# Three changes to the weights of a decoder trunk's feed-forward layers on one core: low parts of plain units by ScalarE and an adding DMA, three plain gate/up pairs instead of four, and one order of sections for both layers

## The chip, the core and the metric

The kernel runs on one core of one Trainium2 chip. The time is the device time of one execution in microseconds (us); the time before is the median of three. The engines are TensorE (PE in the profile, its weight loads PEld), VectorE (DVE), ScalarE (ACT), GpSimd (POOL) and SyncE (SP, which issues DMAs here). SBUF is the on-chip memory of 128 partitions, PSUM the one that TensorE writes, in eight banks of 512 float32 per partition here.

## The reference

The input is x, 512 tokens of 1024 channels, float32. Two layers follow, each a mixer and a dense SwiGLU feed-forward layer, each with an RMS norm ahead and a residual addition behind; a last norm ends it. The mixer of layer 0 is dilated causal attention (24 heads of 128 in three groups), that of layer 1 is causal pooling over 2, 4, 8 and 16 positions in four channel groups. Cut to the part that the change touches:

```
def swiglu_ffn(h, w_gate_up, w_down):          # D_MODEL = 1024, D_FF = 2816
    gu = h @ w_gate_up
    gate, up = gu[..., :D_FF], gu[..., D_FF:]
    return (jax.nn.silu(gate) * up) @ w_down
x = x + swiglu_ffn(rmsnorm(x, ffn_norm[i]), w_ffn_gate_up[i], w_ffn_down[i])
```
and, of the pooling mixer, its input projection `u = h @ w_in` (1024 x 1024).

## The kernel before

**Numbers.** Each float32 operand is split into a high part, rounded to the matmul type fp32r, and a low part, the rest. A product then takes three matmuls: high weight with high and with low data, low weight with high data (L312, L313, L315 for plain products; L444 to L446 for the others). The helper `split` (L91, L92) makes both parts: ScalarE copies the high part, VectorE subtracts it from the value for the low part.

**Weights.** Everything that streams in is planned ahead in three queues: `loads`, `steps`, `units`. A `Plain` unit loads up to 1024 columns by SyncE into one of four `raw` buffers and splits them into one of five `w` buffers (high and low half side by side). A `Pair` unit (Strassen-like, seven products for a 2 x 2 block product) loads two `raw` and one `rawhalf`, adds a block to one of them by an adding DMA from GpSimd's queue (L159), and fills three `w` and one `half` buffer, with two more sums on VectorE (L175, L176). `pump` issues what the rings have room for; it is called behind each product, so a unit is split when the one five places before it in the ring has been used up.

**Products.** A plain product (`Product`) takes 8 chunks of 128 rows with three matmuls of 512 columns each. A product of a pair (`seven`, `chained`) takes seven block products of 4 chunks with three matmuls of 256 columns. In `chained` four of the block products go into a PSUM bank that ScalarE copies out before the next one is added to it (L518, L522, L526, L534).

**The feed-forward layer** (`ffn`). There are 22 chunks of 128 hidden channels. `gate_up(j)` makes chunk j: the first NPLAIN = 4 by two plain products (`plain_pair`), the rest by seven products (`strassen_pair`). During the plain pairs `prepare(k)` (k = 0 to 3) makes the sums and differences of the normed input that the later pairs need, in VectorE and ScalarE. PARTS tells in which sections the second matrix (FF2) is applied: (first, end, block). A section with block is a block product of `chained` form over weights `w_dblock`; one without is plain, eight products of end - first chunks, weights `w_down`. Layer 0 has a plain section of 6 chunks and two blocks of 8, so it ends with a block; layer 1 has a plain section of 2, two blocks of 8, and a plain section of 4 at the end. A section's results are added to x by `down`; behind the last one `note` makes the next norm's operands (ScalarE the high part L376, VectorE the low part L377) and the squares (ScalarE L365, sum L367).

**The norms.** `finish` completes two leading products, whose weights are thereby used up, then calls `rstd`: TensorE sums the squares (L394), VectorE scales (L397), GpSimd takes the power -1/2 (L400, two instructions); TensorE goes on with half a product and then spreads the result (L407). The pooling layer's additions of squares are GpSimd's (`square(..., nc.gpsimd)`), and its input projection comes as eight plain units `w_pin`.

**Order.** Which instruction comes first on an engine's queue is decided when the program is built; the source gives each its dependences and a place. DMAs issued by GpSimd stand in its queue among its arithmetic.

Of the kernel before, what the change touches and what calls it, by code (L numbers as in the profile page):

```python
# [8 lines left out]
F32 = mybir.dt.float32  # L9
F32R = mybir.dt.float32r  # L10
AF = mybir.ActivationFunctionType
OP = mybir.AluOpType
# [3 lines left out]
P = 128  # L16
S = 512
# [19 lines left out]
NF = 4  # L37
H2 = S // 2
K2 = KC // 2
NPLAIN = 4  # L40
WARM = 6
NSOLO = 3
PARTS = {0: ((0, 6, False), (6, 14, True), (14, 22, True)), 1: ((0, 2, False), (2, 10, True), (10, 18, True), (18, 22, False))}
ENDS = 5
BACK = {"blocks": 3, "sums": 7}
BUFS = {"w": 5, "half": 2, "raw": 4, "rawhalf": 2}
# [9 lines left out]
def units_of(n):  # L56
    return (n,) if n <= KC else (n // 2, n - n // 2)
# [3 lines left out]
PIN_ORDER = (6, 7, 4, 5, 2, 3, 0, 1)  # L61
# [3 lines left out]
def trunk(ctx: ExitStack, tc: tile.TileContext, xT, xN, norms, w_first, w_qk, w_qkp, w_v0, w_v0p, w_v12, w_out, w_pair, w_down, w_dblock, w_pin, w_pgrp,  # L65
          consts, ident_in, invcnt_in, outT, outR):
    nc = tc.nc
# [22 lines left out]
    def split(hi, lo, v):  # L90
        nc.scalar.activation(hi, v, AF.Copy)  # L91
        nc.vector.tensor_tensor(lo, v, hi.bitcast(F32), op=OP.subtract)  # L92
# [27 lines left out]
    class Plain:  # L120


        def __init__(self, *srcs, shift=0):
            self.srcs, self.n, self.w, self.shift = srcs, sum(src.shape[-1] for src in srcs), None, shift
            loads.append((self, {"raw": 1}, self.load))
            steps.append((self, "w", self.split))

# [6 lines left out]

        def split(self):
            self.w = Held("w", self.shift)
            split(*(t[:, :self.n] for t in self.w.t), self.raw.t[:, :self.n])
            self.raw.done()

    class Pair:  # L140
# [64 lines left out]
    def pairs(*srcs, shift=LINE // 4, back=False):  # L205

        these = [Pair(src, shift, back) for src in srcs]
        for parts in zip(*(p.steps() for p in these)):
            steps.extend(parts)
        units.append((these,))  # L210

    def share(n, *srcs, shift=0):
        unit = Plain(*srcs, shift=shift)
        each = unit.n // n
        units.extend([(unit, i * each, each, i == n - 1) for i in range(n)])

    def plain_gu(layer, j):
        src = w_pair[layer, j]
        share(1, src[:, S:3 * S])
        share(1, src[:, 3 * S:], src[:, :S])  # L220

    def plain(*srcs):
        for src in srcs:
            share(1, src)

    for h in range(HEADS):
        if h == 0:
# [13 lines left out]

    def ffn_plan(layer):
        j = 0
        for i, (first, end, block) in enumerate(PARTS[layer]):
            while j < min(max(end + block, NPLAIN), FC):
                if j < NPLAIN:
                    plain_gu(layer, j)
                else:
                    pairs(w_pair[layer, j], shift=0, back=True)
                j += 1  # L250
            if block:
                for m in range(K2):
                    pairs(w_dblock[sum(p[2] for l in range(layer) for p in PARTS[l]) + sum(p[2] for p in PARTS[layer][:i]), m],
                          shift=0, back=True)
            else:
                sizes = units_of(end - first)
                step = D // (sizes[0] * P) if len(sizes) == 1 else 1
                for m in range(0, KC, step):
                    o = first * P
                    for n in sizes:  # L260
                        share(step, *[w_down[layer, q, :, o:o + n * P] for q in range(m, m + step)],
                              shift=LINE // 4 * (layer == 1 and end == FC and m + step > KC - ENDS))
                        o += n * P

    ffn_plan(0)
    plain(*[w_pin[m] for m in PIN_ORDER])
    ffn_plan(1)

    class Share:
# [80 lines left out]
    def give(key):  # L350
        del taken[held.pop(key)]
# [6 lines left out]
    def product(layer):  # L358
        return Product(KC, stream(layer)).add(range(KC)).p
# [223 lines left out]
    with tc.tile_pool(name="opool", bufs=1) as opool:  # L583
        early = opool.tile([P, HEADS, S], F32R, tag="o", name="early")
        with tc.tile_pool(name="apool", bufs=1) as apool:
# [253 lines left out]
            H, T, o = {}, {}, []  # L839
# [99 lines left out]
            for c in range(2):  # L939
                p = product(0)  # L940
# [69 lines left out]
    with tc.tile_pool(name="fpool", bufs=2) as fpool:  # L1010
# [13 lines left out]
        def ffn(layer, nxt, lead, row):  # L1024
# [3 lines left out]
            def gu():  # L1028
                return lead.pop(0).p if lead else product(op)

            def plain_pair(j, up):
                pg = gu()
                gt = ftile("gt")
                nc.vector.tensor_mul(gt, pg, row)
                prepare(j)
                pu = gu()
                if j == NPLAIN - 1:
                    for k in range(KC):
                        give((op, k))
                nc.vector.tensor_mul(up, pu, row)  # L1040
                nc.scalar.activation(gt, gt, AF.Silu)
                nc.vector.tensor_mul(up, up, gt)

            T = {}

# [84 lines left out]
                nc.vector.scalar_tensor_tensor(u[:, :H2], left, -1.0, gt[:, :H2], op0=OP.mult, op1=OP.mult)  # L1130

            def gate_up(j, ahead):
                first, block = next((p[0], p[2]) for p in PARTS[layer] if p[0] <= j < p[1])
                u = tmp.tile([P, S], F32, tag="sq", name="u", bufs=3) if block or ahead else ftile("up")
                i, odd = (j - first) // 2, j % 2
                if j < NPLAIN:
                    plain_pair(j, u)
                elif block and odd and j == FC - 1:
                    strassen_pair(u, later(operands, i, U["even"]), later(operands_right, i, u))
                else:  # L1140
                    strassen_pair(u)
                if j == FC - 1:
                    for key in [key for key in held if key[0] == "t"]:
                        give(key)
                if ahead and not block:
                    U["later"] = j, u
                elif not block:
                    keep(j, u)
                elif not odd:
                    U["even"] = u  # L1150
                elif j == FC - 1:
                    operands_left(i, u)
                else:
                    late.extend([later(operands, i, U["even"]), later(operands_right, i, u), later(operands_left, i, u)])
# [4 lines left out]
                    note(nxt, m)  # L1159

            j = 0
            for first, end, block in PARTS[layer]:
# [181 lines left out]
        t = total(t, add(2, 1, end(2, 1, range(HALF // 2, HALF), f)))  # L1344
# [3 lines left out]
        t = total(t, add(3, 1, f))  # L1348
# [101 lines left out]
```

## Time and profile before

| what | value |
|---|---|
| time, median of 3 (lowest, highest) | 1194.25 us (1193.57, 1194.67) |
| the profiled execution's own time | 1194.79 us |
| its span, first to last instruction | 1192.6 us |
| granted TensorE clock | 0.998 of full speed |
| DMA queue of SyncE | 141.98 MB, 35.2% of 16 engines' span |
| DMA queue of GpSimd | 44.58 MB, 23.2% of 16 engines' span |
| splits into `w` (L91 on ScalarE, L92 on VectorE) | 299 each |

In the order of the span: attention to about 430 us, its output projection to 481, feed-forward layer 0 to 797, pooling to 870, feed-forward layer 1 and the last norm to the end. Busy shares are of the whole span. A matmul's duration in the timeline is modelled and overlaps the next one's, so matmuls are priced from start to start. Releasers of waits are inferred from semaphores. "x36 | 43.7, 1213 | 361.5" in a group's row means 36 instructions, 43.7 us busy, 1213 ns in the mean, and 361.5 us of the engine's idle time before them.

### The profile page before, as it was taken

Reading aid. Unit: us, or ns where it says so; the run is one execution under the profiler, and the core shown is the slowest. Engines: PE = TensorE matmul, PEld = TensorE weight load, DVE = VectorE, ACT = ScalarE, POOL = GpSimd, SP = SyncE. Lnnn points to the kernel's source line nnn. Section 1 sums busy time; section 2 is a strip of 40 time slices with the busy share of each in tenths; the row PEclk is TensorE's granted clock in tenths of the full one; section 3 lists DMA queues with packets and bytes.
Section 4 is the critical chain, followed back from the end, with each engine's and each line's share of the span. In section 5 each row is a group of like instructions: output and inputs, shape, how many; then the busy total and the mean of one; then the engine's idle time right before and its main releaser. Section 6 shows DMA issues by size and latency. Waiting matters only on the chain.

```text
span 1192.6 us, 24834 instructions
## 1 busy us (share of the span) xinstructions
PE 1182.2 (99%) x9936; PEld 1120.0 (94%) x9936; DVE 995.0 (83%) x1712; ACT 680.8 (57%) x1214; POOL 147.5 (12%) x137
## 2 busy tenths in 40 slices
PE   9999999999999999999999999999999999999997
PEld 7889999999999988898999999998789999999997
DVE  6978898889788856795799889997989998898875
ACT  6445564555456544562677567763455776676553
POOL 1111211111111000101111111100310111111100
PEclk9999999999999999999999999999999999999999
DMA  8346656665766534336677777753153777777732
GB/s 285 118 107 159 158 152 161 171 159 149 189 146 163 158 140 126 88 110 161 160 198 190 187 200 197 192 176 124 54 123 91 192 196 200 197 187 196 193 89 71
DMA packets 73363, 188.40 MB, mean 158 GB/s; under 512 B 7312, under 2 KB 9504, under 8 KB 73248
## 3 DMA queue, kind: packets, MB, share of 16 engines
q1 hardware_dynamic: 50400, 141.98, 35.2%
q0 software_dynamic: 22704, 44.58, 23.2%
q8 instruction: 77, 1.26, 0.4%
q14 instruction: 38, 0.31, 0.1%
q10 hardware_dynamic: 144, 0.26, 0.1%
HBM read 184.70 MB, written 2.10 MB: 157 GB/s over the span
## 4 chain that ended last, share of the span: by engine, by line
PE 91%; DVE 5%; issue 2%; ACT 1%; DMA 0%; POOL 0%; DVEq 0%; POOLq 0%; SPq 0%; ACTq 0%
PE ps L444 19%; PE ps L445 18%; PE ps L446 18%; PE ps L312 7%; PE ps L313 7%; PE ps L315 7%; PE ps L615 2%; PE ps L617 2%; PE ps L616 2%; PE ps L905 2%; DVE w L92 2%; PE ps L827 1%; PE ps L699 1%; DVE far L92 1%; PE ps L821 1%
## 5 line engine op out<-in xcount | busy, mean ns | idle before, releaser
L91 ACT ACTIVATE w<-raw 128x1024 fp32r<-128x1024 f32 (+1 forms) x299 | 313.6, 1056 | 211.7 <-PE ps L446 69.0
L92 DVE TENSOR_TENSOR w<-raw,w 128x1024 fp32r<-128x1024 f32 (+1 forms) x299 | 361.7, 1214 | 59.0 <-ACT w L91 55.3
L444 PE MATMUL ps<-far,w 128*128 128x256 f32 x916 | 251.9, 275 | 0.1
L445 PE MATMUL ps<-far,w 128*128 128x256 f32 x916 | 252.0, 275 | 0.0
L446 PE MATMUL ps<-far,w 128*128 128x256 f32 x916 | 251.8, 275 | 0.0
L444 PE MATMUL ps<-near,w 128*128 128x256 f32 x632 | 178.5, 282 | 0.4 <-ACT first L526 0.4
L445 PE MATMUL ps<-near,w 128*128 128x256 f32 x632 | 174.8, 277 | 0.0
L446 PE MATMUL ps<-near,w 128*128 128x256 f32 x632 | 174.8, 277 | 0.0
L444 PEld LDWEIGHTS ps<-far,w 128*128 128x128 f32 x916 | 171.8, 188 | 0.6 <-ACT first L526 0.5
L445 PEld LDWEIGHTS ps<-far,w 128*128 128x128 f32 x916 | 172.0, 188 | 0.2
L446 PEld LDWEIGHTS ps<-far,w 128*128 128x128 f32 x916 | 172.0, 188 | 0.0
L444 PEld LDWEIGHTS ps<-near,w 128*128 128x128 f32 x632 | 118.9, 188 | 1.3 <-ACT first L526 0.9
L445 PEld LDWEIGHTS ps<-near,w 128*128 128x128 f32 x632 | 118.8, 188 | 0.0
L446 PEld LDWEIGHTS ps<-near,w 128*128 128x128 f32 x632 | 118.8, 188 | 0.0
L313 PE MATMUL ps<-near,w 128*128 128x512 f32 (+1 forms) x284 | 106.4, 375 | 1.3 <-DVE near L377 1.3
L312 PE MATMUL ps<-near,w 128*128 128x512 f32 (+1 forms) x284 | 107.0, 377 | 0.0
L315 PE MATMUL ps<-near,w 128*128 128x512 f32 (+1 forms) x284 | 106.2, 374 | 0.0
L159 POOL DMA_DIRECT2D raw<-w_pair x36 | 43.7, 1213 | 361.5 <-DMA raw<-w_pair 135.1
L313 PEld LDWEIGHTS ps<-near,w 128*128 128x128 f32 x284 | 53.4, 188 | 11.4 <-DVE near L377 2.1
L312 PEld LDWEIGHTS ps<-near,w 128*128 128x128 f32 x284 | 53.4, 188 | 9.4
L315 PEld LDWEIGHTS ps<-near,w 128*128 128x128 f32 x284 | 53.3, 188 | 9.5
L91 ACT ACTIVATE half<-rawhalf 128x512 fp32r<-128x512 f32 x81 | 51.0, 631 | 14.7 <-PE ps L446 12.5
(319 smaller groups left out, 2731.2 us busy)
## 6 DMA issues: line engine op xcount, KB each, us to landing
raw<-w_pair SPq DMA_DIRECT2D x80, 512.0 KB, 4.4
raw<-w_qkp SPq DMA_DIRECT2D x36, 512.0 KB, 4.2
raw<-w_pair POOLq DMA_DIRECT2D x36, 512.0 KB, 7.4
raw<-w_dblock SPq DMA_DIRECT2D x32, 512.0 KB, 4.3
raw<-w_v SPq DMA_DIRECT2D x18, 512.0 KB, 4.1
raw<-w_qkp POOLq DMA_DIRECT2D x18, 512.0 KB, 7.3
rawhalf<-w_pair SPq DMA_DIRECT2D x36, 256.0 KB, 5.0
raw<-w_dblock POOLq DMA_DIRECT2D x16, 512.0 KB, 7.5
```

Of the source, the lines that this page charges most:

```text
L91: nc.scalar.activation(hi, v, AF.Copy)
L92: nc.vector.tensor_tensor(lo, v, hi.bitcast(F32), op=OP.subtract)
L159: nc.gpsimd.dma_start(self.b.rearrange("p (a c) -> p a c", a=2), self.src[:, None, 3 * n:].to_broadcast([P, 2, n]), accum_op=OP.add)
L312: nc.tensor.matmul(self.p[:, cols], w[0][:, s], mh[:, cols], start=self.done == 0, stop=False)
L313: nc.tensor.matmul(self.p[:, cols], w[0][:, s], ml[:, cols], start=False, stop=False)
L315: nc.tensor.matmul(self.p[:, cols], w[1][:, s], mh[:, cols], start=False, stop=self.done == self.n)
L444: nc.tensor.matmul(dst, w.t[0][:, c], th, start=k == 0 and not on, stop=False, skip_group_check=on)
L445: nc.tensor.matmul(dst, w.t[0][:, c], tl, start=False, stop=False, skip_group_check=on)
L446: nc.tensor.matmul(dst, w.t[1][:, c], th, start=False, stop=k == n - 1, skip_group_check=on)
L615: nc.tensor.matmul(o, mh, wh, start=k == 0, stop=False)
L616: nc.tensor.matmul(o, mh, wl, start=False, stop=False)
L617: nc.tensor.matmul(o, ml, wh, start=False, stop=k == K2 - 1)
```

## The change

It does three things at once. NPLAIN becomes 3; `prepare` for k = 2 moves behind the second plain pair, and for k = 3 into the third. PARTS becomes the one order that layer 1 had, for both layers. And a plain unit may be `lean`: then ScalarE writes the high part, ScalarE writes its negative into the low half, and GpSimd issues one DMA per source that adds the weight from memory to it. Lean are the plain gate/up units (two a pair, the second with two sources), the plain FF2 units (four sources of 256 columns in the section of 2 chunks, two of 512 in that of 4) and the eight units of `w_pin`: 12, 12 and 8 units. The attention's plain units stay as they were.

```
-NPLAIN = 4
+NPLAIN = 3
-PARTS = {0: ((0, 6, False), (6, 14, True), (14, 22, True)), 1: ((0, 2, False), (2, 10, True), (10, 18, True), (18, 22, False))}
+PARTS = ((0, 2, False), (2, 10, True), (10, 18, True), (18, 22, False))
...
         def split(self):
             self.w = Held("w", self.shift)
-            split(*(t[:, :self.n] for t in self.w.t), self.raw.t[:, :self.n])
+            hi, lo = (t[:, :self.n] for t in self.w.t)
+            if self.lean:
+                nc.scalar.activation(hi, self.raw.t[:, :self.n], AF.Copy)
+                nc.scalar.activation(lo, hi.bitcast(F32), AF.Copy, scale=-1.0)
+                o = 0
+                for src in self.srcs:
+                    nc.gpsimd.dma_start(lo[:, o:o + src.shape[-1]], src.bitcast(F32R), accum_op=OP.add)
+                    o += src.shape[-1]
+            else:
+                split(hi, lo, self.raw.t[:, :self.n])
             self.raw.done()
...
     def plain_gu(layer, j):
         src = w_pair[layer, j]
-        share(1, src[:, S:3 * S])
-        share(1, src[:, 3 * S:], src[:, :S])
+        share(1, src[:, S:3 * S], lean=True)
+        share(1, src[:, 3 * S:], src[:, :S], lean=True)
...
-                        share(step, *[w_down[layer, q, :, o:o + n * P] for q in range(m, m + step)],
+                        share(step, *[w_down[layer, q, :, o:o + n * P] for q in range(m, m + step)], lean=True,
...
-    plain(*[w_pin[m] for m in PIN_ORDER])
+    plain(*[w_pin[m] for m in PIN_ORDER], lean=True)
...
                 nc.vector.tensor_mul(gt, pg, row)
-                prepare(j)
+                prepare((0, 1, 3)[j])
                 pu = gu()
...
                 nc.scalar.activation(gt, gt, AF.Silu)
                 nc.vector.tensor_mul(up, up, gt)
+                if j == 1:
+                    prepare(2)
```
The rest of the diff passes `lean` on and drops the layer's index from PARTS.

More of the change, by code (lines that the diff above doesn't have):

```diff
@@ L120, in trunk, with __init__ @@
     class Plain:
-        def __init__(self, *srcs, shift=0):
-            self.srcs, self.n, self.w, self.shift = srcs, sum(src.shape[-1] for src in srcs), None, shift
+        def __init__(self, *srcs, shift=0, lean=False):
+            self.srcs, self.n, self.w, self.shift, self.lean = srcs, sum(src.shape[-1] for src in srcs), None, shift, lean
             loads.append((self, {"raw": 1}, self.load))
@@ L210, in pairs, with share @@
         units.append((these,))
-    def share(n, *srcs, shift=0):
-        unit = Plain(*srcs, shift=shift)
+    def share(n, *srcs, shift=0, lean=False):
+        unit = Plain(*srcs, shift=shift, lean=lean)
         each = unit.n // n
@@ L218, in plain_gu, with plain @@
         src = w_pair[layer, j]
-        share(1, src[:, S:3 * S])
-        share(1, src[:, 3 * S:], src[:, :S])
-    def plain(*srcs):
+        share(1, src[:, S:3 * S], lean=True)
+        share(1, src[:, 3 * S:], src[:, :S], lean=True)
+    def plain(*srcs, lean=False):
         for src in srcs:
-            share(1, src)
+            share(1, src, lean=lean)
     for h in range(HEADS):
@@ L243, in ffn_plan @@
         j = 0
-        for i, (first, end, block) in enumerate(PARTS[layer]):
+        for i, (first, end, block) in enumerate(PARTS):
             while j < min(max(end + block, NPLAIN), FC):
@@ L252, in ffn_plan @@
                 for m in range(K2):
-                    pairs(w_dblock[sum(p[2] for l in range(layer) for p in PARTS[l]) + sum(p[2] for p in PARTS[layer][:i]), m],
+                    pairs(w_dblock[sum(p[2] for p in PARTS) * layer + sum(p[2] for p in PARTS[:i]), m],
                           shift=0, back=True)
@@ L1132, in gate_up @@
             def gate_up(j, ahead):
-                first, block = next((p[0], p[2]) for p in PARTS[layer] if p[0] <= j < p[1])
+                first, block = next((p[0], p[2]) for p in PARTS if p[0] <= j < p[1])
                 u = tmp.tile([P, S], F32, tag="sq", name="u", bufs=3) if block or ahead else ftile("up")
@@ L1161, in ffn @@
             j = 0
-            for first, end, block in PARTS[layer]:
+            for first, end, block in PARTS:
                 while j < min(max(end + block, NPLAIN), FC):
@@ L1399 @@
                                .transpose(0, 1, 2, 4, 3, 5).reshape(K2, 2, P, 2, (end - first) // 2 * P))
-                       for layer in PARTS for first, end, block in PARTS[layer] if block])
+                       for layer in range(2) for first, end, block in PARTS if block])
     pg = v["w_pool_group"][0].reshape(2, 2, 2, P, 2, P).transpose(0, 3, 1, 4, 2, 5).reshape(2, P, D)
```

## The prediction, made before the change had run

> **What bounds the kernel now.** I read the page first, for the engines' shares and the chain; then the waits of TensorE; then the timeline of TensorE at the places where it waits; then the table by stretches.
>
> ```profile
> span 1192.6 us, 24834 instructions
> PE 1182.2 (99%) x9936; PEld 1120.0 (94%) x9936; DVE 995.0 (83%) x1712; ACT 680.8 (57%) x1214; POOL 147.5 (12%) x137
> PE 91%; DVE 5%; issue 2%; ACT 1%; DMA 0%; POOL 0%; DVEq 0%; POOLq 0%; SPq 0%; ACTq 0%
> ```
> ```profile
> PE ps L313 <- DVE near L377: 1.3, 2, 0.7
> ...
> PE ps L444 <- ACT first L526: 0.4, 1, 0.4
> ```
> TensorE is busy 99% of the span, and no wait of it for another engine adds up to over 1.3 us. VectorE (DVE) at 83% is no bound over the whole, so most of the time that the change takes off it is worth nothing. But two stretches are tight:
>
> ```profile
> 485.00:515.00 30.00, 30.00 (x136) 24.88 (x135) 28.95 (x48) 17.55 (x27) 1.26 (x1) 1.00 0.28 73
> 773.00:795.00 22.00, 21.64 (x184) 21.24 (x184) 21.12 (x33) 17.14 (x32) 0.00 (x0) 1.00 0.60 186
> 838.00:854.00 16.00, 14.65 (x64) 11.51 (x63) 15.96 (x29) 7.75 (x12) 4.11 (x3) 1.00 0.28 89
> 870.00:913.00 43.00, 43.00 (x200) 35.91 (x199) 41.00 (x67) 22.18 (x34) 3.77 (x4) 1.00 0.43 105
> ```
> (Columns: the stretch, its length, busy us of PE, PEld, DVE, ACT, POOL, granted clock, DMA share, GB/s.) In the last block of layer 0 (773 to 795) and in the pooling layer (838 to 854) VectorE is full and TensorE falls short of the stretch by 0.36 and 1.35 us. At the starts of the two feed-forward layers (485 and 870) VectorE is over 95% full, yet TensorE keeps going. So there are two things to gain: fewer or shorter matmuls, and these holes.
>
> **Part 1: one gate/up pair per layer goes from plain to seven products.** The profile's matmul durations overlap, so I price by start to start.
>
> ```profile
> 479.64 0.39 PE L312 MATMUL ps<-near,w 128*128 128x512 f32 x1
> ...
> 480.77 0.39 PE L315 MATMUL ps<-near,w 128*128 128x512 f32 x1
> 99.83 0.28 PE L617 MATMUL ps<-w,near 128*128 128x256 f32 x1
> ...
> 106.18 0.28 PE L616 MATMUL ps<-w,near 128*128 128x256 f32 x1
> ```
> The first two rows stand five steps apart: 1.13 / 5 = 0.226 us for 512 columns. The other two stand 56 steps apart: 6.35 / 56 = 0.1134 us for 256 columns. A plain pair is 2 products x 8 chunks x 3 = 48 matmuls of 512: 10.87 us. A pair by seven products is 7 x 4 x 3 = 84 of 256: 9.53 us. That saves 1.34 us a layer, **2.7 us** in both. The Trainium skill (TensorE: Matmul & The Clock Gate, "Wait — 56ns, not 53.3ns?") gives N / 2.4 GHz plus some 2.5 ns from start to start. By it a pair would go from 10.36 to 9.17 us and both layers save 2.4 us, an estimate from that page; the trace's steps are 4 to 5% longer, and the sum goes by them.
>
> VectorE's work moves too. The rows for it:
>
> ```profile
> L92 DVE TENSOR_TENSOR w<-raw,w 128x1024 fp32r<-128x1024 f32 x291 | 354.3, 1221 | 58.0 <-ACT w L91 54.3
> L91 ACT ACTIVATE w<-raw 128x1024 fp32r<-128x1024 f32 x291 | 307.1, 1062 | 201.7 <-PE ps L446 68.1 <-PE ps L315 49.2 <-issue 36.9
> L1157 DVE TENSOR_TENSOR x<-x,ps 128x512 f32<-128x512 f32 x19 | 12.7, 684 | 14.7 <-PE ps L315 14.7
> L530 DVE TENSOR_TENSOR gt<-ps,first 128x256 f32<-128x256 f32 x36 | 15.1, 419 | 10.2 <-PE ps L446 10.1
> L377 DVE SCALAR_TENSOR_TENSOR near<-x,nrm,near 128x512 fp32r<-128x512 f32 x17 | 15.4, 907 | 1.2 <-ACT near L376 1.0
> ```
> A pair by seven products needs three low parts of 1.22 us, a half one and two sums of 512 columns (0.68 each, as L1157's) and some five evictions of 0.42, 7.8 us; a plain pair has three multiplications of 512 columns, 2.1 us. The four operand preparations now fall into three plain pairs (32.6 us) instead of four. From the stretch 870 to 913 VectorE's load there loses five plain low parts (6.1 us) and a pair's 2.1 us, and TensorE's time loses 10.9 us: about 41 us of work against 43 us of matmuls up to the first pair by seven products, as tight as the same place is now. I take no new wait there and no gain.
>
> **Part 2: layer 0 takes layer 1's sections.** Sections of 2 and 4 chunks have 8 x (2 + 4) x 3 = 144 matmuls of 512 columns, as the section of 6 has now, so TensorE gains nothing. VectorE gets 8 more additions into x, 5.5 us, spread beside matmuls. What goes is the ending by a block, whose last products write x, its norm operands and squares while the block's copies run:
>
> ```profile
> 772.73 0.28 PE L446 MATMUL ps<-far,w 128*128 128x256 f32 x1
> 773.36 0.39 PE L444 MATMUL ps<-near,w 128*128 128x256 f32 x1 [0.35 <-ACT first L526]
> ```
> A step of 0.63 us instead of 0.11. With the smaller hitches at 783 and 793 and the slow steps behind each I count 1.2 us up to 795. A plain ending takes 2.7 us of matmuls for each x against 2.3 us on VectorE (0.68 for x, 0.91 for the low operand, 0.68 for the square's sum), and layer 1 has that order without a hole. I take all of the **1.2 us**.
>
> **Part 3: the low parts of 32 plain units by ScalarE and an adding DMA.** VectorE loses 38 low parts of plain feed-forward and pooling units (44 us), gets 6 for the two new pairs, and is covered nearly everywhere. It pays in the pooling layer:
>
> ```profile
> 847.99 1.22 DVE L92 TENSOR_TENSOR w<-raw,w 128x1024 fp32r<-128x1024 f32 x1
> 849.12 1.41 DVE L1248 SCALAR_TENSOR_TENSOR x<-ps,nrm,x 128x512 f32<-128x512 f32 x2
> 850.44 0.68 DVE L92 TENSOR_TENSOR far<-u,far 128x512 fp32r<-128x512 f32 x1
> 851.04 2.44 DVE L377 SCALAR_TENSOR_TENSOR near<-x,nrm,near 128x512 fp32r<-128x512 f32 x2
> 851.28 3.35 POOL L367 TENSOR_TENSOR sq<-sq 128x512 f32<-128x512 f32 x2 [10.27 <-issue]
> 521.88 0.67 PE L444 MATMUL ps<-far,w 128*128 128x256 f32 x2
> ```
> TensorE waits twice for L377 here; with the slow steps behind, 1.9 us. Without the 1.22 us at 847.99 the chain starts earlier. But the two L377 take 2.44 us, against 2 x 0.91 in the mean, beside GpSimd's additions of squares (851.28), and that stays. I take **1.2 us** of the 1.9. The other holes are of the size of the last row's, where two matmuls take 0.51 us to the next start (522.39) instead of 0.23; I count 0.3 us of gain for all of them.
>
> What it adds. ScalarE gets 32 more instructions of 1.06 us; it is at 57%. Most lie in plain sections, where nothing hurries it. Some eight fall into pairs by seven products at the end of each layer's pairs, where TensorE reuses a PSUM bank one product (12 x 0.1134 = 1.36 us) after it was filled, and ScalarE's copy (0.37 us, L518 in the fence after next) must be done by then: a 1.06 us instruction that has just begun makes the copy late by up to 0.4 us. The one such hit that the trace shows is the 0.35 us above. Bounds 0 and 3.2 us; I take **0.8 us**.
>
> The DMAs must land before use. The nearest rows are four issues of plain loads on GpSimd, and the landing of the pairs' adding DMAs (L159):
>
> ```profile
> 413.57 2.22 POOL L966 DMA_DIRECT2D x<-xN  x4 [29.21 <-PE ps L616]
> DMA to landing us min/median/max: 6.3/7.4/10.9
> ```
> A unit costs ScalarE 2.1 us, one to four issues of 0.55 us (2.22 / 4) and some 7 us of landing: 10 to 12. In plain sections the ring of five holds four units ahead, 4 x 5.45 = 21.8 us of matmuls. The tightest is the first unit of the last section:
>
> ```profile
> 1147.74 2.21 ACT L91 ACTIVATE w<-raw 128x1024 fp32r<-128x1024 f32 x2
> 1151.61 0.37 ACT L518 COPY first<-ps 128x256 f32<-128x256 f32 x1 [0.48 <-PE ps L446]
> 1159.51 0.39 PE L312 MATMUL ps<-near,w 128*128 128x512 f32 x1
> ```
> 11.8 us plus two matmuls before the low part is read, against 2.1 + 1.1 + 7.4 = 10.6. It fits, by 1.6 us. DMA work is 4.9 us a plain unit (1.55 to load, 3.3 to add, by the queues' shares below) against 5.45 us of matmuls: hidden.
>
> ```profile
> q1 hardware_dynamic: 50400, 141.98, 35.2%
> q0 software_dynamic: 22704, 44.58, 23.2%
> ```
> **The wait it adds** is on GpSimd: each adding DMA waits there for ScalarE's low part. Behind it on that queue stand the later pairs' adding DMAs, the squares, and the power in each norm, for which TensorE waits. At all three norms concerned, two units come free just before that power:
>
> ```profile
> 480.56 2.01 ACT L91 ACTIVATE w<-raw 128x1024 fp32r<-128x1024 f32 x2 [8.01 <-issue]
> 481.85 2.77 POOL L400 TENSOR_TENSOR rcol<-var,nhalf 128x2 f32<-128x2 f32 x2 [3.44 <-DVE var L397]
> 807.18 1.06 ACT L91 ACTIVATE w<-raw 128x1024 fp32r<-128x1024 f32 x1 [5.24 <-issue]
> 809.67 2.42 POOL L400 TENSOR_TENSOR rcol<-var,nhalf 128x2 f32<-128x2 f32 x2 [40.99 <-DVE var L397]
> 865.21 1.06 ACT L91 ACTIVATE w<-raw 128x1024 fp32r<-128x1024 f32 x1 [2.05 <-PE ps L315]
> 867.68 2.42 POOL L400 TENSOR_TENSOR rcol<-var,nhalf 128x2 f32<-128x2 f32 x2 [2.29 <-DVE var L397]
> 869.69 1.18 PE L407 MATMUL ps<-ident,rcol 128*128 128x128 f32 x8
> ```
> TensorE's spreading product (869.69) starts just as the power ends: no slack. The order on each queue is fixed when the program is built. If it goes by which is ready first, the first unit's DMA (start of the first row of each site + 2.1) comes at 482.7, 809.3 and 867.3: behind the power at the first site, just ahead of it at the other two, for one and two issues. That costs 0 + 0.5 + 0.8, so **1.3 us**. Bounds: 0, and 11.7 in the rival below.
>
> **Sum**, against the profiled execution (1194.8 us, a span of 1192.6 and 2.2 around it): -2.7 - 1.2 - 1.2 - 0.3 + 0.8 + 1.3 = -3.3, so 1191.5; the median lies 0.5 below that execution: **1190.9 us**.
>
> **Rivals.**
> *The norms wait (slower).* If both units' DMAs stand ahead of the power, it waits for four ScalarE instructions and the second unit's issues: at the first site 480.56 + 4.2 + 4 x 0.55 = 487.0 for 481.85, 5.1 us late; at the second 2.6 (one issue); at the third 4.0 (four issues). Together 11.7 instead of 1.3: **1201.3**. It decides wherever the second unit's DMA is queued first, for in source order it is. Speaking against: at none of the sites is that DMA ready before the power. The Trainium skill (Perfetto Trace Analysis, "Tensor Engine Instruction (MATMUL, LD_WEIGHTS)") says that GpSimd's queue is strictly first in, first out, so nothing would let the power pass a DMA that stands ahead of it; no row of this trace shows a power held up so.
> *The DMAs land late.* At the longest landing above (10.9) the tight unit is 1.9 to 2.9 us late, once a layer, up to 5.8: **1196.7**. For: more adding DMAs share the queue. Against: the median.
> *The holes stay.* They are latency, not load: TensorE saves 2.7 and pays 2.1: **1193.7**. For: the slow L377 stays; against: the full VectorE.
> *All holes go, no new waits:* -2.7 - 4.0: **1187.5**.
>
> **How the numbers follow.** Forecast 0.50, norms wait 0.13, late DMAs 0.09, holes stay 0.19, all gain 0.09. About 0.2% (2.4 us) is what a measurement of this kernel can tell from no change. The forecast lies 3.3 us below the median with some 2 us around it, so a seventh of it counts as the same. Faster 0.53, same 0.27, slower 0.20. The range from 1187.2 to 1197.0 leaves out the norms' wait alone.
>
> **What would show it.** Part 1: 72 more matmuls (10008). Part 3: VectorE's L92 on w falls from 299 to 267, its busy time by some 27 us, ScalarE's grows by about 40, GpSimd has 60 more DMAs. The waits of TensorE lose the ACT entry at the end of layer 0 and most of L377's. A wait of the spreading product L407 for GpSimd's power of over 1 us shows the slower rival; a wait of L315 for a DMA into w the late landing. The prediction is wrong if TensorE's holes after 480 us grow at all.

## The result, and the profile after the change

The changed kernel takes **1196.21 us** (median of 22 runs, 1193.98 to 1198.88), the kernel before 1194.26 (22 runs, 1193.52 to 1195.63). The ratio is 1.0015, 95% interval 1.0009 to 1.0021: slower by 2 us. That is small, within the 0.2% that the forecast called no change, but the interval leaves out 1, and the forecast was 1190.9, the other way. The profiled execution took 1196.03 us.

The page of the changed kernel, with the lines that answer to those of before:

```profile
span 1194.3 us, 25131 instructions
...
PE 1182.9 (99%) x10008; PEld 1122.5 (94%) x10008; DVE 970.9 (81%) x1698; ACT 714.2 (60%) x1255; POOL 197.9 (17%) x197
...
PE 86%; DVE 7%; DMA 3%; ACT 2%; issue 2%; POOL 1%; DVEq 0%; POOLq 0%; ACTq 0%; SPq 0%
...
L92 DVE TENSOR_TENSOR w<-raw,w 128x1024 fp32r<-128x1024 f32 x267 | 324.6, 1221 | 47.3 <-ACT w L91 43.9
```
All that the change was to move, it moved: 72 more matmuls (10008), 32 fewer low parts on VectorE (267), VectorE 24 us less busy, ScalarE 33 us more, GpSimd 60 more instructions. Yet VectorE's share of the chain that ended last rose from 5% to 7%, and the DMAs' from nothing to 3%. (Line numbers are 9 to 11 higher than before: L321, L322, L324 were L312, L313, L315; L453 to L455 were L444 to L446; L1049 was L1040; L184 and L185, a pair's sums, were L175 and L176. ScalarE's two instructions of a lean unit are L139 and L140. In e5 and e9 most lines are 6 higher still.)

TensorE's waits from 480 us on, and the same stretches as before (columns as in the prediction):

```profile
PE ps L321 <- DVE u L1049: 1.8, 1, 1.8
PE ps L453 <- ACT first L527: 1.2, 4, 0.4
PE ps L453 <- ACT first L535: 0.4, 1, 0.4
PE ps L322 <- DVE near L386: 0.2, 1, 0.2
```
```profile
773.00:795.00 22.00, 22.00 (x109) 18.23 (x108) 12.57 (x22) 18.82 (x26) 6.14 (x8) 1.00 1.08 276
838.00:854.00 16.00, 15.75 (x70) 12.73 (x69) 12.28 (x20) 9.31 (x14) 6.99 (x7) 1.00 0.83 177
870.00:902.20 32.20, 30.35 (x130) 24.67 (x129) 32.12 (x56) 17.92 (x29) 8.68 (x9) 0.97 0.59 118
```
The old holes are smaller: 773 to 795 lost 0.36 us and now nothing, 838 to 854 lost 1.35 and now 0.25. At the start of layer 1, where TensorE kept going before, it now falls 1.85 us short, VectorE is busy for the whole stretch, and the granted clock is 0.97.

The stages, from the first matmul of each norm's column sums to the next (L394 before, L403 after), tell where the 1.7 us of span are:

| stage (us) | before | after | after, four plain pairs (e4) | best (e10) |
|---|---|---|---|---|
| feed-forward layer 0 | 327.3 | 327.8 | 326.3 | 325.3 |
| pooling | 58.1 | 56.5 | 57.5 | 55.9 |
| feed-forward layer 1 | 309.9 | 314.1 | 310.0 | 309.3 |
| last norm and output | 16.2 | 15.1 | 15.6 | 15.6 |

Layer 1 loses 4.2 us where 1.34 were to be gained; layer 0 loses 0.5 where 2.5 were to be gained; the rest gains 2.8 together, and 0.2 were gained ahead of these stages.

**The wait.** VectorE in the changed kernel, from its first eviction of layer 1 to its last one of the third plain pair, and TensorE beside the latter:

```profile
870.08 0.69 DVE L1043 TENSOR_TENSOR gt<-ps,row 128x512 f32<-128x512 f32 x1 [4.20 <-ACT row L422]
...
897.97 1.22 DVE L92 TENSOR_TENSOR w<-raw,w 128x1024 fp32r<-128x1024 f32 x1
899.11 0.68 DVE L1049 TENSOR_TENSOR u<-ps,row 128x512 f32<-128x512 f32 x1
```
```profile
897.62 0.39 PE L324 MATMUL ps<-near,w 128*128 128x512 f32 x1
899.85 0.50 PE L321 MATMUL ps<-near,w 128*128 128x512 f32 x1 [1.85 <-DVE u L1049]
900.19 0.52 PE L322 MATMUL ps<-near,w 128*128 128x512 f32 x1
900.50 0.63 PE L324 MATMUL ps<-near,w 128*128 128x512 f32 x1
```
L1049 takes the pair's second product out of PSUM. VectorE comes to it at 899.11, having worked without a pause since 870.08. TensorE is by then seven FF2 products past that pair, and its eighth needs the PSUM bank.

**The clock.** Steps of 512 columns behind the wait go to 0.43 us (900.50 to 900.93) from 0.23. The stretches around it (granted clock is the third number from the right):

```profile
897.00:900.00 3.00, 1.15 (x6) 0.65 (x5) 3.00 (x5) 1.88 (x2) 1.20 (x1) 1.00 0.04 15
900.00:904.00 4.00, 4.00 (x16) 3.46 (x17) 4.00 (x7) 1.47 (x2) 0.00 (x0) 0.57 0.84 179
```
For 4 us the clock is 0.57: some 1.7 us lost (4 x 0.43) on top of the 1.85.

### The profile page after: what moved, and what is told of

Same layout as the page of the kernel before. It is cut to its first block, busy times and chain, and to the rows that moved or that the text cites. A ratio compares the mean times of both kernels' runs of the same rounds, so it can differ in the third digit from the quotient of the medians.

```text
span 1194.3 us, 25131 instructions
## 1 busy us (share of the span) xinstructions
PE 1182.9 (99%) x10008; PEld 1122.5 (94%) x10008; DVE 970.9 (81%) x1698; ACT 714.2 (60%) x1255; POOL 197.9 (17%) x197
## 3 DMA queue, kind: packets, MB, share of 16 engines
q0 software_dynamic: 31600, 62.41, 32.1%
## 4 chain that ended last, share of the span: by engine, by line
PE 86%; DVE 7%; DMA 3%; ACT 2%; issue 2%; POOL 1%; DVEq 0%; POOLq 0%; ACTq 0%; SPq 0%
PE ps L453 19%; PE ps L455 18%; PE ps L454 18%; PE ps L321 6%; PE ps L324 6%; PE ps L322 6%; PE ps L624 2%; PE ps L625 2%; PE ps L626 2%; DMA raw<-w_pair 2%; PE ps L914 2%; DVE far L92 1%; PE ps L836 1%; DVE w L92 1%; PE ps L708 1%
## 5 line engine op out<-in xcount | busy, mean ns | idle before, releaser
L91 ACT ACTIVATE w<-raw 128x1024 fp32r<-128x1024 f32 x267 | 281.5, 1062 | 162.5 <-PE ps L455 73.8
L92 DVE TENSOR_TENSOR w<-raw,w 128x1024 fp32r<-128x1024 f32 x267 | 324.6, 1221 | 47.3 <-ACT w L91 43.9
L453 PE MATMUL ps<-far,w 128*128 128x256 f32 x944 | 261.3, 277 | 1.8 <-ACT first L527 1.2
L454 PE MATMUL ps<-far,w 128*128 128x256 f32 x944 | 260.0, 276 | 0.0
L455 PE MATMUL ps<-far,w 128*128 128x256 f32 x944 | 259.8, 276 | 0.0
L453 PEld LDWEIGHTS ps<-far,w 128*128 128x128 f32 x944 | 177.6, 188 | 4.1 <-ACT first L527 2.7
L453 PE MATMUL ps<-near,w 128*128 128x256 f32 x640 | 180.3, 282 | 0.0
L454 PEld LDWEIGHTS ps<-far,w 128*128 128x128 f32 x944 | 177.6, 188 | 0.1
L455 PEld LDWEIGHTS ps<-far,w 128*128 128x128 f32 x944 | 177.4, 188 | 0.0
L454 PE MATMUL ps<-near,w 128*128 128x256 f32 x640 | 177.0, 277 | 0.0
L455 PE MATMUL ps<-near,w 128*128 128x256 f32 x640 | 176.9, 276 | 0.0
L453 PEld LDWEIGHTS ps<-near,w 128*128 128x128 f32 x640 | 120.5, 188 | 0.4
L454 PEld LDWEIGHTS ps<-near,w 128*128 128x128 f32 x640 | 120.3, 188 | 0.0
L455 PEld LDWEIGHTS ps<-near,w 128*128 128x128 f32 x640 | 120.3, 188 | 0.0
L321 PE MATMUL ps<-near,w 128*128 128x512 f32 (+1 forms) x300 | 113.5, 379 | 1.9 <-DVE u L1049 1.8
L322 PE MATMUL ps<-near,w 128*128 128x512 f32 (+1 forms) x300 | 112.9, 376 | 0.2 <-DVE near L386 0.2
L324 PE MATMUL ps<-near,w 128*128 128x512 f32 (+1 forms) x300 | 113.0, 377 | 0.0
L321 PEld LDWEIGHTS ps<-near,w 128*128 128x128 f32 x300 | 56.4, 188 | 12.6 <-DVE u L1049 2.3
L322 PEld LDWEIGHTS ps<-near,w 128*128 128x128 f32 x300 | 56.6, 189 | 10.7 <-DVE near L386 0.7
L324 PEld LDWEIGHTS ps<-near,w 128*128 128x128 f32 x300 | 56.5, 188 | 10.4
```

Source lines behind the costliest of these rows:

```text
L321: nc.tensor.matmul(self.p[:, cols], w[0][:, s], mh[:, cols], start=self.done == 0, stop=False)
L322: nc.tensor.matmul(self.p[:, cols], w[0][:, s], ml[:, cols], start=False, stop=False)
L324: nc.tensor.matmul(self.p[:, cols], w[1][:, s], mh[:, cols], start=False, stop=self.done == self.n)
L453: nc.tensor.matmul(dst, w.t[0][:, c], th, start=k == 0 and not on, stop=False, skip_group_check=on)
L454: nc.tensor.matmul(dst, w.t[0][:, c], tl, start=False, stop=False, skip_group_check=on)
L455: nc.tensor.matmul(dst, w.t[1][:, c], th, start=False, stop=k == n - 1, skip_group_check=on)
```

## The experiments

**Theory A:** with three plain pairs VectorE's work at the start of a feed-forward layer outlasts TensorE's, and all else follows from that. **Rival B:** the lean low parts cost more than they save, in ScalarE's queue and by late adding DMAs. The last column is (ratio - 1) x 1194.3; the ratio is to the kernel before timed beside each, so kernels are compared by this column.

| run | plain pairs | sections | lean | median us (lowest, highest) | ratio to before, 95% | us |
|---|---|---|---|---|---|---|
| the change | 3 | new | yes | 1196.21 (1193.98, 1198.88) | 1.0015 (1.0009, 1.0021) | +1.8 |
| e1_lean_only | 4 | old | yes | 1193.81 (1192.68, 1195.45) | 0.9996 (0.9988, 1.0005) | -0.5 |
| e2_parts_only | 4 | new | no | 1192.13 (1191.72, 1193.14) | 0.9981 (0.9973, 0.9990) | -2.3 |
| e3_three_plain_only | 3 | old | no | 1200.31 (1198.82, 1202.52) | 1.0051 (1.0038, 1.0063) | +6.1 |
| e4_lean_parts | 4 | new | yes | 1192.36 (1191.70, 1192.81) | 0.9981 (0.9972, 0.9990) | -2.3 |
| e5_lean_pairs | 3 | new | and pairs 3, 4 | 1196.30 (1195.66, 1197.87) | 1.0019 (1.0010, 1.0028) | +2.3 |
| e6_three_chunks | 3 | first of 3 chunks | yes | 1194.53 (1194.10, 1196.53) | 1.0003 (0.9994, 1.0012) | +0.4 |
| e7_squares | 4 | new | yes | 1190.75 (1190.51, 1191.50) | 0.9969 (0.9958, 0.9980) | -3.7 |
| e8_last_dve | 4 | new | not the last section | 1190.61 (1190.00, 1191.15) | 0.9970 (0.9958, 0.9981) | -3.6 |
| e9_lean_pairs_1 | 3 | new | and pairs 3, 4 of layer 1 | 1192.48 (1191.42, 1193.15) | 0.9985 (0.9976, 0.9994) | -1.8 |
| e10_four_best | 4 | new | as e8, squares as e7 | **1188.78** (1188.35, 1189.47) | 0.9954 (0.9940, 0.9967) | -5.5 |
| e11_three_best | 3 | new | as e10 | 1193.00 (1191.08, 1195.08) | 0.9990 (0.9981, 0.9999) | -1.2 |
| e12_no_lean | 4 | new | no, squares as e7 | 1190.81 (1190.44, 1191.85) | 0.9970 (0.9959, 0.9982) | -3.6 |

### The three parts by themselves

**e1_lean_only**: the changed kernel with the old values of the two constants and `prepare(j)` as before.
```
-NPLAIN = 3
-PARTS = ((0, 2, False), (2, 10, True), (10, 18, True), (18, 22, False))
+NPLAIN = 4
+PARTS = {0: ((0, 6, False), (6, 14, True), (14, 22, True)), 1: ((0, 2, False), (2, 10, True), (10, 18, True), (18, 22, False))}
```
Expected: 

> The kernel before with the low parts of plain units by ScalarE and the adding DMA alone: four plain pairs, the old sections. Theory A (VectorE falls behind at the start of the feed-forward layers because three plain pairs leave it too little time; the trace after shows TensorE waiting 1.8 us for the eviction of the third pair's up product and then 2.0 us at half clock): the lean path itself costs little, VectorE gets five low parts less there, the hole in the pooling layer shrinks as it did after (1.9 to 0.5), ScalarE's late copies cost 0.5: 1192.5 to 1193.5. Rival B (the lean path costs, by ScalarE's, GpSimd's and the DMAs' load): as slow as the changed kernel or slower, 1196 or more.

**e2_parts_only**: the kernel before with one constant changed.
```
-PARTS = {0: ((0, 6, False), (6, 14, True), (14, 22, True)), 1: ...
+PARTS = {0: ((0, 2, False), (2, 10, True), (10, 18, True), (18, 22, False)), 1: ...
```
Expected: 

> Of the change the sections alone: layer 0 takes layer 1's, the low parts stay with VectorE and the plain pairs stay four. Step 2 of the prediction by itself: the wait of 1.2 us in layer 0's last section goes and nothing takes its place, 1192.8 to 1193.3 (ratio 0.9988 to 0.9992); the difference between the change with four plain pairs and the lean low parts alone asks for the same, 1.4 us. The rival: the short sections of layer 0 need the lean low parts, because VectorE has to split twice as many small units there: 1194.3 or more.

**e3_three_plain_only**: the kernel before with NPLAIN = 3 and the moved preparations.
```
-NPLAIN = 4
+NPLAIN = 3
...
-                prepare(j)
+                prepare((0, 1, 3)[j])
...
+                if j == 1:
+                    prepare(2)
```
Expected: 

> The kernel before with three plain pairs alone (and the preparations moved as in the change); low parts by VectorE, the old sections. Theory A: TensorE saves 2.7 us, but VectorE has the whole load at the start of both layers, so the stall there is longer than after the change, with the half clock behind it: 1197 to 1203, and TensorE waits for VectorE before the first pair by seven products in both layers. Rival B: no lean path, so no stall: 1191 to 1192.

**e4_lean_parts**: the changed kernel with four plain pairs.
```
-NPLAIN = 3
+NPLAIN = 4
...
-                prepare((0, 1, 3)[j])
+                prepare(j)
...
-                if j == 1:
-                    prepare(2)
```
Expected: 

> The changed kernel with four plain pairs (each with its own preparation): lean path and the one order of sections stay. Theory A: the stall at the start of layer 1's feed-forward part and the half clock behind it go (4 us), most of the 2.3 us at the start of layer 0's as well, TensorE pays 2.7 us more: 1191.5 to 1193.5. Rival B: the stall stays, 1197 to 1199.

The lean low parts alone cannot be told from no change: 0.3 us above what A expected, 2.2 below B's 1196. The sections alone gain 2.3 us, more than either side expected. Both together gain 2.3. Three plain pairs alone lose 6.1 us, and on top of the other two 4.1. So the loss belongs to the plain pairs. The lean low parts seem to soften it: layer 1, whose sections are the same in both, takes 316.0 us in e3's profile and 314.1 in the change's. TensorE's waits in e3, then in e4 (e3's profiled execution, 1202.39 us, is 2.1 above its median):

```profile
PE ps L312 <- DVE u L1040: 2.9, 1, 2.9
PE ps L444 <- ACT first L518: 1.6, 1, 1.6
PE ps L313 <- DVE near L377: 1.4, 2, 0.7
PE ps L444 <- ACT first L526: 1.3, 3, 0.6
PE ps L444 <- ACT far L91: 1.1, 1, 1.1
```
```profile
PE ps L322 <- DVE near L386: 1.3, 1, 1.3
PE ps L453 <- ACT first L527: 0.5, 2, 0.3
```
e3 has the wait for the last plain eviction (L1040 there) at 2.9 us in layer 1, and behind it waits for ScalarE's copies, the longest 1.6 us at 930. In layer 0 TensorE waits 1.1 us for the operand `far`, at 509 us, where the products by seven start. The kernel before and e4, both with four plain pairs, have none of these but the pooling layer's wait (L377, in e4 L386) and waits of at most 0.4 us for copies.

### Giving VectorE time at that place

**e5_lean_pairs**: the changed kernel, with the two tiles `b` and `l` of pairs 3 and 4 lean in both layers; **e9_lean_pairs_1**: in layer 1 alone.
```
-            split(*(t[:, :raw.shape[-1]] for t in w.t), raw)
+            hi, lo = (t[:, :raw.shape[-1]] for t in w.t)
+            if src is None:
+                split(hi, lo, raw)
+            else:
+                nc.scalar.activation(hi, raw, AF.Copy)
+                nc.scalar.activation(lo, hi.bitcast(F32), AF.Copy, scale=-1.0)
+                nc.gpsimd.dma_start(lo, src.bitcast(F32R), accum_op=OP.add)
...
-                    pairs(w_pair[layer, j], shift=0, back=True)
+                    pairs(w_pair[layer, j], shift=0, back=True, lean=j < NPLAIN + 2)                    # e5
+                    pairs(w_pair[layer, j], shift=0, back=True, lean=layer == 1 and j < NPLAIN + 2)     # e9
```
Expected of e5: 

> The changed kernel, with the low parts of two more tiles lean (the first and the last block of pairs 3 and 4 of each layer, the first two by seven products): they leave VectorE for ScalarE and adding DMAs, some 3.7 us of VectorE's work in the stretch that starts a feed-forward layer. Theory A (the three plain pairs give VectorE less matmul time than it has work there): the wait of 1.85 us at 897 us and the half clock behind it shrink below 1 us together, 1192.0 to 1193.5, so 2.5 to 4 us less than the changed kernel. Theory B (the lean low parts are what costs: ScalarE's queue, late adding DMAs): there is more of them now, 1196.5 to 1198.

By its time, 0.2 us below B's range, e5 spoke for B. Its stages say otherwise: layer 1 took 310.1 us instead of 314.1, and layer 0 331.8 instead of 327.8. What layer 0 lost is one wait of TensorE; GpSimd's queue shows what it waited for (first fence the waits, second the timeline of GpSimd):

```profile
PE ps L461 <- DMA w<-w_pair: 4.2, 1, 4.2
PE ps L327 <- DVE u L1055: 0.7, 1, 0.7
```
```profile
517.82 1.20 POOL L168 DMA_DIRECT2D raw<-w_pair  x1 [21.09 <-ACT w L91]
518.81 1.16 POOL L180 DMA_DIRECT2D w<-w_pair  x1
```
The low part's adding DMA was issued at 518.81, right behind a pair's own adding DMA, and landed at 529.65, 10.8 us later; TensorE wanted it at 525.3. That is the forecast's rival of late DMAs, in a place that this experiment made. The wait for the plain eviction (L1055 in e5) shrank to 0.7 us.

Expected of e9: 

> The changed kernel with the low parts of two tiles of pairs 3 and 4 lean in layer 1 alone. With both layers so, layer 1 took 310.1 us instead of the changed kernel's 314.1, and layer 0 lost 4.35 us in one wait for an adding DMA. Theory A (VectorE is short of time between the row and the first product by seven): layer 1 keeps its 310 us and layer 0 the changed kernel's 328: 1192.0 to 1193.5. Theory B (the gain of one layer was made by the loss of the other, or lean copies cost as much as they save): 1195.5 to 1197.

It came out as A had it: 1192.48, and layer 1 at 310.1 us, with 0.7 us of wait for the last plain eviction. Moving two low parts of each of two pairs off VectorE, in this one place, gains 3.6 us.

**e6_three_chunks**: the changed kernel with a longer first section, so that TensorE has more to do before it needs the bank.
```
-PARTS = ((0, 2, False), (2, 10, True), (10, 18, True), (18, 22, False))
+PARTS = ((0, 3, False), (3, 11, True), (11, 19, True), (19, 22, False))
...
-                i, odd = (j - first) // 2, j % 2
+                i, odd = (j - first) // 2, (j - first) % 2
```
Expected: 

> The changed kernel with sections of 3, 8, 8 and 3 chunks instead of 2, 8, 8 and 4, in both layers: the same matmuls, but 5.4 us of plain FF2 products more ahead of the first pair by seven products, 5.4 less at the end. Theory A: VectorE's lag of some 2 to 4 us at that place is covered, so the stall and the half clock go in layer 1 and most of the 2.3 us in layer 0: 1190.5 to 1192.5. Rival B: nothing changes, 1195 to 1197.

It came out between the two, at 1194.53: A expected too much. The wait at 897 us and its slow clock went, but VectorE's lag came out later. ScalarE's timeline in layer 0 of e6:

```profile
542.23 1.06 ACT L91 ACTIVATE w<-raw 128x1024 fp32r<-128x1024 f32 x1 [3.30 <-DMA raw<-w_pair]
...
544.23 0.35 ACT L527 COPY first<-ps 128x256 f32<-128x256 f32 x1
```
A `raw` buffer comes free late because VectorE's sums on it (L184, L185) are late (the first ends at 525.38, and the load into its buffer is issued at 525.45); so the next pair's adding DMA is late (issued at 532.66, landed 9.4 us later); so ScalarE stands 3.3 us before a split, and behind it stands the copy L527, for which TensorE waits 1.6 us.

### The other holes, and the best version

**e7_squares** and **e8_last_dve**, each e4 with one line changed:
```
-                square(3, m, nc.gpsimd)
+                square(3, m)                # e7
...
-  ... for q in range(m, m + step)], lean=True,
+  ... for q in range(m, m + step)], lean=end < FC,          # e8
```
Expected of e7: 

> The change with four plain pairs, and the running sum of squares in the pooling layer added by VectorE instead of GpSimd (7 additions, about 0.69 us each on VectorE). Theory A2: in the hole of 1.4 us at 850 us VectorE's L92 and L386 take 1.8 us instead of 0.7 only because GpSimd's addition runs beside them; without it the hole falls to 0.4 us or less: 1191.0 to 1191.8. Theory B2: VectorE is simply the engine with the longest queue there, and 5 us more of work make the hole longer: 1192.4 to 1194.

Expected of e8: 

> The change with four plain pairs, and the low parts of each layer's last feed-forward section split by VectorE again. The two waits of 0.43 us for the first copy (at 767 and 1150 us) stand behind two ScalarE copies each of a unit of that section. Theory A3: they go, with the small losses behind them, and VectorE has room there: 1191.3 to 1191.9. Theory B3: VectorE lacks the time in the last section, and its tail waits come back as in the kernel before: 1192.4 to 1194.

The pooling layer in e4 (timeline, VectorE and GpSimd), then in e7 (VectorE):

```profile
848.29 3.01 POOL L376 TENSOR_TENSOR sq<-sq 128x512 f32<-128x512 f32 x2 [0.46 <-ACT sq L374]
848.38 1.79 DVE L92 TENSOR_TENSOR far<-u,far 128x512 fp32r<-128x512 f32 x1
850.09 1.76 DVE L386 SCALAR_TENSOR_TENSOR near<-x,nrm,near 128x512 fp32r<-128x512 f32 x1
```
```profile
849.28 0.75 DVE L386 SCALAR_TENSOR_TENSOR near<-x,nrm,near 128x512 fp32r<-128x512 f32 x1
849.94 0.69 DVE L376 TENSOR_TENSOR sq<-sq 128x512 f32<-128x512 f32 x1
850.54 0.69 DVE L92 TENSOR_TENSOR far<-u,far 128x512 fp32r<-128x512 f32 x1
```
With the additions on VectorE its two instructions take 0.69 and 0.75 us instead of 1.79 and 1.76, and the hole of 1.4 us is gone, though VectorE has more to do. e8 loses the two waits for the first copy, which stood behind ScalarE's lean copies:

```profile
765.31 1.04 ACT L140 ACTIVATE w<-w 128x1024 fp32r<-128x1024 f32 x1
766.26 0.61 ACT L91 ACTIVATE near<-up 128x512 fp32r<-128x512 f32 x1
766.78 0.35 ACT L527 COPY first<-ps 128x256 f32<-128x256 f32 x1
```
(e4; TensorE's next matmul started 0.43 us late by it.) Both gained a little more than expected.

**e10_four_best** has both edits, **e11_three_best** both with three plain pairs, **e12_no_lean** is e2 with the edit of e7.

Expected of e10: 

> The change with four plain pairs, the last section of each layer split by VectorE, and the pooling layer's sum of squares added by VectorE. If the two holes that these remove are separate, their gains add (1.6 and 1.75 us against the change with four plain pairs): 1188.6 to 1189.6. If VectorE's added work in one comes back as a wait in the other: 1190.0 to 1191.

Expected of e11: 

> The same with three plain pairs: the changed kernel with the last section split by VectorE and the sum of squares added by VectorE. Theory A: the third plain pair's absence costs VectorE's time at the start of a layer whatever is mended elsewhere, so that it stands 3 to 4.5 us above the same kernel with four plain pairs, 1192 to 1193.5. Theory B: what the three plain pairs lost was lost in the queues that these edits clear, and they are worth their 1.3 us a layer: 1186 to 1188.

Expected of e12: 

> The kernel before with layer 0's sections changed and the sum of squares added by VectorE: no lean low parts at all, four plain pairs. Theory A: the lean low parts outside the last section are worth their share of the small holes, 1.3 to 1.7 us, so that this kernel stands that much above the one with them, 1190.2 to 1191. Theory B: on an engine that is not the bound they are worth nothing once the pooling hole is gone: within 0.4 us of the kernel with them, 1188.8 to 1189.6.

e11 and e12 went as A had them, and e10 as two separate holes would have it. e10 has no wait of TensorE from 450 us on that the view of waits lists, and takes 5.5 us less than the kernel before and 7.3 less than the change. The lean low parts are worth some 2 us there (e12 against e10, whose runs do not overlap), a little more than A's 1.3 to 1.7. They are worth something only with the last section left out: with it they gain 0.0 (e4 against e2) and 0.1 (e7 against e12), without it 1.3 (e8 against e2, whose runs do not overlap either). Three plain pairs still cost 4.2 us (e11 against e10).

## Why the prediction was wrong, point by point

**The step that failed** is the end of Part 1: "about 41 us of work against 43 us of matmuls up to the first pair by seven products, as tight as the same place is now. I take no new wait there and no gain." The forecast had just taken 8.2 us off VectorE and 10.9 off TensorE, and went on with the numbers from before the subtraction; subtracted, they are 32.8 against 32.1, full. And what counts is not the stretch but the queue up to one instruction, the last plain eviction. VectorE in the kernel before, its first and its last plain eviction of layer 1, and then TensorE's eighth FF2 product:

```profile
871.54 0.69 DVE L1034 TENSOR_TENSOR gt<-ps,row 128x512 f32<-128x512 f32 x1 [2.64 <-ACT row L413]
...
902.17 0.68 DVE L1040 TENSOR_TENSOR u<-ps,row 128x512 f32<-128x512 f32 x1
```
```profile
910.17 0.39 PE L312 MATMUL ps<-near,w 128*128 128x512 f32 x1
```
Before, VectorE needs from its first eviction (871.54) to the end of its last one (902.85) 31.3 us; after, from 870.08 to 899.79, 29.7. It got only 1.6 us shorter, where the forecast had taken off 8.2: a pair's three multiplications and two low parts into `w` go (five are left three), but the four preparations stay, and the sums of the next pair (L184, L185) and two more low parts of the last preparation (L92 on `far`) come in front. From the same event TensorE has 38.6 us of matmuls before, up to its eighth FF2 product (910.17), the first that needs that bank. After, it has 27.8, up to 897.85, where the wait begins. So 7.3 us of slack became a deficit of 1.9, the wait seen. (Two and a half of the plain products are done before the row, the norm's factor for each token, is known, and give VectorE no time at all: one plain pair less takes 10.9 us from 38.6, not from 43.)

In layer 0 of the changed kernel the same eviction came in time. VectorE's first and last plain eviction there, and TensorE's eighth FF2 product:

```profile
485.83 0.69 DVE L1043 TENSOR_TENSOR gt<-ps,row 128x512 f32<-128x512 f32 x1 [4.27 <-ACT row L422]
...
508.00 0.68 DVE L1049 TENSOR_TENSOR u<-ps,row 128x512 f32<-128x512 f32 x1
```
```profile
513.60 0.39 PE L321 MATMUL ps<-near,w 128*128 128x512 f32 x1
```
TensorE has 27.8 us again, but VectorE's queue up to the eviction is 22.9 us. Most of the last preparation, the next pair's two sums and a low part into `w`, 5.8 us that stand in front of the eviction in layer 1 (893.30 to 899.11), stand behind it here. So the wait took both: the shorter work of TensorE and that order on VectorE's queue. Layer 1 with layer 0's order was not tried.

**The saving of matmuls** (2.7 us) is in the counts, but cannot be seen in a time: three plain pairs cost 4.1 us on top of the other two parts, 6.8 us away from the forecast's -2.7. In the trace of after: 1.85 of wait and 1.7 of clock at 897 us; 1.2 in two waits of layer 1 behind ScalarE's copies (924.9, 937.9), which follow VectorE's lag and are gone in e9; and some 2.3 in small holes of layer 0 from 514 to 545 us, where 0.4 were lost before. That is 7.0. By the stages of the two profiled executions the feed-forward layers lose 5.5 us against e4, so 8.2 beside the 2.7 of matmuls; some 1.2 of it is in no wait that I can name. The pooling layer and the last stage take 1.5 us less than in e4; 1.0 of that is the pooling hole below, and the rest is open.

**The sections** (-1.2): right in sign, and worth -2.3 alone; layer 0's stage in e2 is 325.8 us for 327.3, the rest is spread over places that show no wait.

**The pooling hole** (-1.2 of 1.9): it did shrink to 0.5 in the changed kernel, but not for the reason given, so that the number came near was luck. With the same lean low parts a hole of 1.4 us is left in e1, e4 and e6: its cause is GpSimd's additions, which the forecast named and left 0.7 us for. e7 showed it. In the changed kernel only one addition ran ahead of the wait (849.62 to 850.95), and only one instruction of VectorE was slow there (1.79 us at 849.71).

**ScalarE's copies** (+0.8): 0.55 us in each layer (a wait of 0.43 and a slow step of 0.11 at 768 and 1155 us), 1.1 in both, so the size was nearly right, and e8's gain confirms the place.

**The norms** (+1.3, and the rival of 11.7): neither happened. GpSimd's timeline in the changed kernel at the third norm:

```profile
865.96 1.37 POOL L409 TENSOR_TENSOR rcol<-var,nhalf 128x2 f32<-128x2 f32 x2 [1.89 <-DVE var L406]
867.28 1.79 POOL L143 DMA_DIRECT2D w<-w_pair  x2
```
The adding DMAs stand behind the power, at the other two norms as well (481.66 and 809.43). Nor is the forecast's "no slack" borne out: the spreading product starts 3.2 us after the column sums at all three norms, before and after, without a wait, and here 1.0 us after the power's row ends. "The prediction is wrong if TensorE's holes after 480 us grow at all" was the right test.

## What to carry to other kernels

When a change takes time from the bound engine, look for the engine that was only just keeping up, and compare its queue up to the instruction that frees a buffer with the other's work up to where it needs that buffer, both counted from the same event. Put what a helper loses and what it must still do before that point in two columns: here one lost 10.9 us and the other 1.6, and in the layer where 5.8 us of work stood behind that instruction instead of in front of it there was no wait. Test the parts of a change alone: of three, one was good, one showed no gain until its last section was left out, and one was bad in every company.

## What the runs showed of the hardware beyond that

**The clock after a wait.** TensorE's steps took about twice their time for 3.2 to 3.4 us behind the waits of 1.85 us (the change, 900.50 to 903.71), 2.9 (e3, 906.46 to 909.86) and 4.2 (e5, 530.51 to 533.92), and did not behind those of 1.3 (e1, e4) or 1.6 (e3, e6). It is not fixed by the wait alone. The profiled execution of e11 waited 1.9 us for L1049 and kept the full clock:

```profile
897.00:900.00 3.00, 1.99 (x11) 1.73 (x12) 3.00 (x6) 0.71 (x3) 0.88 (x1) 1.00 0.39 72
900.00:904.00 4.00, 4.00 (x38) 4.00 (x37) 4.00 (x7) 1.74 (x4) 0.00 (x0) 1.00 0.95 208
```
It was the fastest of e11's eleven (1191.08). Over those, the five with a mean granted clock of 0.999 took 1192.1 us in the mean and the four with 0.997 took 1194.1; of the change's 22, six at 0.999 took 1194.9 and twelve at 0.997 or less 1196.7. The change ranges over 4.9 us and e11 over 4.0; without the wait, e4 (eleven runs) and e10 (five) range over 1.1, but e1 (eleven) over 2.8, so the clock need not be all of it. The Trainium skill (TensorE: Matmul & The Clock Gate, "Part 1: The HAM clock gate (the "warmup" mystery)") tells of a free-running activity window of some 3.4 us; a window that does not start with the kernel would make the same wait hit or miss, as the two traces do, but its rule of an idle window of 3.4 us is longer than the 1.85 us that sufficed here. That the clock makes the wide ranges was read from the records, not tried by itself.

**VectorE beside GpSimd.** Two-input instructions of 512 columns on VectorE took 1.76 to 1.79 us while GpSimd added two tiles, and 0.69 to 0.75 us without it. The Trainium skill (SBUF — State Buffer, "Who interferes with whom") says that a VectorE instruction with two inputs in SBUF contends with a GpSimd instruction that reads SBUF; the runs agree, and e7 prices it at 1.4 us of 1192.
